# A macaron encoder layer on eight cores: entry norm's sums placed inside the preceding FFN, 256-query exponentials, split down tiles, and a different order of the last stages

## The chip, the cores and the metric

The kernel runs on the 8 cores of one Trainium2 chip. Each core does the whole layer for 2 of the 16 sequences, and the cores do not talk to each other. The metric is the device time of the slowest core, in microseconds (us).

Most executions of a kernel here agree within 0.3% (before the change, 14 of 20 lie from 3009.4 to 3017.6 us). Only fast executions are compared. Even among those, one die is sometimes slightly disturbed (in a fast execution of `a_xycut` one die is at 0.982 to 0.984 and the other at 0.989 to 0.992), and the slowest of eight cores is a noisy statistic. So I also use the **undisturbed die mean**: over all executions of a kernel, I take each die whose four cores all had a granted clock of at least 0.983, and average the spans of its cores. For the three kernels whose last mixer runs without filler to its end (before, `z_xycut`, `a_order`; in the kernel before 75.1 to 78.5 us of it are at a clock of 0.50) the limit is 0.971. I chose both limits after looking at the data; single dies of one kernel then lie within 14 us of each other. n is the number of dies.

The experiments ran in five sets of rounds, and each set ran the kernel before again. Its own die mean differs between the sets, from 3000.1 to 3008.7 us, so a difference of less than about 9 us between kernels of different sets is not shown by the die means alone. Where it matters I also give the difference from the kernel before in the same set.

## The reference, cut to what matters

```python
x = x + 0.5 * swiglu(rms_norm(x), ...)          # FFN1, 1024 -> 2816 -> 1024
proj = rms_norm(x) @ w_in                       # mixer: one projection for all heads
fox = fox_attention(...)                        # 8 heads of 64, causal, F_t - F_s added to the logits
gla = gla_chunk_causal(...)                     # 4 heads, chunked linear attention
x = x + concat(fox, gla) @ w_out
x = x + 0.5 * swiglu(rms_norm(x), ...)          # FFN2
y = rms_norm(x)
```

The input is 16 x 2048 x 1024 in float32. A core handles its 4096 frames as 8 groups (0 to 7) of 512 frames. For each group there is one FFN1, one mixer and one FFN2.

## The kernel before: the parts that matter

Everything is kept transposed: x of one group is 8 tiles of 128 channels x 512 frames, float32, 2 MB, loaded by DMA and later stored as y (another 2 MB). There are three such buffers. A matmul's sum lands in a PSUM bank, and the program lets the next sum start in it only after another engine has emptied (evacuated) it. The weights are not kept on the core: every FFN streams them from memory again, as 352 tiles of 512 KB and 256 of 352 KB in a whole run (sizes after conversion to bf16). Small helpers record all operations in a list. A planner with a model of durations then fixes the order in which each engine runs them, and inserts the semaphore waits. That order is static: an instruction that waits holds up everything behind it on its engine (TensorE for 10.86 us at the entry sums below).

The mixer's attention is slow for TensorE alone, because each pair of matmuls needs an exponential in between (in the bare stretch below, ScalarE is busy for 19.65 of 20 us in which TensorE runs 42 matmuls). So the planner fills it with matmuls of an FFN that is independent of it. An operation has a level, and lower levels are preferred.

```python
def ffn(f, xb, after):
    for half in range(2):
        for cl in range(NC2):                    # 11 chunks of 128 hidden columns
            DMA("pool", ("wgu", wb), wgu[:, wb, :], wgu_d[f][half * NC2 + cl], ...)
            MM(banks[bg][:], [(w4[:, 0, k, :], hF[:, k, :]) for k in range(8)], ...)   # gate
            ...                                  # up, tanh, products: act[:, cl, :]
        for d in range(8):                       # 8 down tiles
            DMA("pool", ("wd", wb), wd[:, wb, :], wd_d[f][half * 8 + d], ...)
            b = nxt("fb", 2)                     # two PSUM banks in turn
            MM(banks[b][:], [(wd[:, wb, c * 128:(c + 1) * 128], act[:, c, :]) for c in range(NC2)], ...)
            STT(x_sb[:, xb, d, :], banks[b][:], 0.25, x_sb[:, xb, d, :], ...)          # add to x
            ...

def ffn1_pre(tg):                                # "entry norm" of a group
    DMA("sp", ("x", xb), x_sb[:, xb, ...], x_d[tg], 1 << 21, ...)
    for k in range(8):
        norm_sq(xb, k, sqM, "sqM", b, k == 7, 0) # square on ScalarE, sum on TensorE
    norm_rstd(rstdF, "rstdF", b, 0)
# ... (mixer, with the attention over 8 heads) ...
ffn1_pre(0)
ffn1(0)
for n in range(NTG):
    if n + 1 < NTG:
        ffn1_pre(n + 1)
    if n >= 1:
        ffn2_pre(n - 1)
    mixer(n)                                     # filled by what follows
    if n >= 1:
        ffn2(n - 1)
    if n + 1 < NTG:
        ffn1(n + 1)
ffn2_pre(NTG - 1)
ffn2(NTG - 1)
```

The softmax here doesn't subtract the row's maximum and nothing guards it: scores larger than these inputs give would overflow.

## Time and profile before

| | before |
|---|---|
| time, median of the first 6 executions | 3013.79 us (3009.38 to 3303.41) |
| undisturbed die mean | 3004.5 us (n = 34; three sets of rounds. Over all five: 3003.1, n = 65) |
| granted clock, mean of a core | 0.973 to 0.976 |
| TensorE busy (profiled core) | 2814 of 3009 us |

TensorE is the limit. At the pace of the FFN matmuls in the trace (0.216 us from start to start for 512 columns) all matmuls together take about 2604 us (an estimate from this pace and the number of columns), which is the floor that no reordering can lower. The rest is what the change aims at.

First, lines of the profile's page (slowest core, core 0): busy time by engine, granted clock and DMA share in 40 slices of the span in tenths, and groups of instructions (count, busy us, mean ns, then the idle time just before them and what ended most of it).

```profile
PE 2813.9 (94%) x13344; PEld 1236.1 (41%) x13344; DVE 1439.4 (48%) x2007; ACT 1251.6 (42%) x3187; POOL 518.2 (17%) x1019
...
PEclk9999989999999999999999999999999999999599
DMA  9978667589776787766877878868887568775066
...
L298 PE MATMUL bank<-hF,wgu 128*128 128x512 bf16 x5632 | 1287.4, 381 | 24.7 <-DMA wgu<-wgu 13.2
...
L298 PE MATMUL bank<-act,wd 128*128 128x512 bf16 x2816 | 641.1, 380 | 19.5 <-DVE act L335 16.2
```

The third digit from the end of the clock string is a 5: one slice of the run, 75 us, is at half clock, and the DMA share of the same slice is 0. FFN matmuls (`hF,wgu`) hardly wait for their weights, 13.2 us in all.

The windows view of the same core shows what that slice is (busy us and instruction count of each engine, then granted clock, DMA share, GB/s):

```profile
2780.00:2800.00 20.00, 19.99 (x42) 4.07 (x41) 6.16 (x4) 19.65 (x76) 1.66 (x4) 0.50 0.00 1
2800.00:2820.00 20.00, 19.99 (x41) 4.03 (x40) 4.04 (x2) 19.64 (x76) 1.67 (x4) 0.50 0.00 0
```

The last mixer has outlived its only filler, and TensorE, at a granted clock of 0.50, and ScalarE run the bare attention, both nearly full by the profile (whose ends of matmuls are modelled).

Now the waits of TensorE, on core 3, which I use because it is an ordinary core (us in total, times, longest):

```profile
PE bank L298 <- ACT sqM L323: 64.5, 25, 11.1
...
PE bank L298 <- DVE act L335: 17.5, 18, 2.0
PE bank L298 <- DVE hM L338: 16.0, 8, 2.3
PE bank L298 <- DMA wgu<-wgu: 11.7, 19, 2.0
```

The largest wait is for the squares of the entry norm (`sqM`). The timeline of TensorE on core 3 shows two of its places (start, duration, then in brackets the idle time before and what ended it):

```profile
42.73 1.10 PE L298 MATMUL bank<-sqM,onesD 128*128 128x512 bf16 x2 [10.86 <-ACT sqM L323]
...
47.99 2.31 PE L298 MATMUL bank<-hF,wgu 128*128 128x512 bf16 x7
...
640.88 1.10 PE L298 MATMUL bank<-sqM,onesD 128*128 128x512 bf16 x2 [10.55 <-ACT sqM L323]
```

At the start, TensorE's queue stands 10.86 us at the entry sums of group 1 although group 0's FFN could run; its first FFN matmul comes at 48 us. At 641 us, in the middle of the program, it stands 10.55 us because x of the next group has not landed (ScalarE's square before it waits 10.80 us for that DMA): the planner placed the sums where its model had the data ready.

### The profile page before, as it was taken

What the parts mean: (1) busy time and instruction counts of PE and PEld (TensorE: products, weight loads), DVE (VectorE), ACT (ScalarE), POOL (GpSimd) and SP (SyncE); (2) the same over time, 40 slices, a digit from 0 to 9 for tenths busy, and PEclk for the clock granted to TensorE, in tenths of its full rate; (3) what the DMA queues carried; (4) which work ended last, traced back from release to release, by engine and by line L of the source; (5) the groups of instructions that cost most, each with busy time, mean ns of one, the idle gap of its engine ahead of it and who ended that gap; (6) DMA issues with size and microseconds to landing.
All of it is one profiled execution on the core that took longest, in us unless ns stands there. A gap on an engine that the chain in (4) does not pass through costs nothing.

```text
span 3008.9 us, 40414 instructions; the slowest of 8 cores (2995.9 to 3008.9 us)
## 1 busy us (share of the span) xinstructions
PE 2813.9 (94%) x13344; PEld 1236.1 (41%) x13344; DVE 1439.4 (48%) x2007; ACT 1251.6 (42%) x3187; POOL 518.2 (17%) x1019
## 2 busy tenths in 40 slices
PE   5999989989999999999999899999999999999988
PEld 1445334334443344433444334533445334443233
DVE  2345745633455444553446635364445554454233
ACT  2132433631248522587324323175132762348711
POOL 1111311211112111111112111122111221111110
PEclk9999989999999999999999999999999999999599
DMA  9978667589776787766877878868887568775066
GB/s 184 144 127 138 115 106 125 97 163 146 122 127 114 137 140 134 119 113 118 141 128 129 157 132 136 138 106 160 142 135 130 88 127 147 131 126 101 13 105 116
DMA packets 118057, 380.24 MB, mean 126 GB/s; under 512 B 13391, under 2 KB 13536, under 8 KB 116960
## 3 DMA queue, kind: packets, MB, share of 16 engines
q0 software_dynamic: 106176, 344.07, 70.1%
q1 hardware_dynamic: 11680, 33.58, 3.4%
q8 instruction: 115, 1.88, 0.2%
q14 instruction: 86, 0.70, 0.1%
HBM read 704.84 MB, written 16.78 MB: 240 GB/s over the span
## 4 chain that ended last, share of the span: by engine, by line
PE 73%; DMA 14%; DVE 6%; issue 4%; ACT 3%; SPq 0%; DVEq 0%; POOL 0%; ACTq 0%; POOLq 0%
PE bank L298 73%; DMA mixw_t<-mixw 6%; DMA wgu<-wgu 4%; DMA x_sb<-x 2%; DMA y<-x_sb 1%; DVE hM L338 1%; DVE x_sb L338 1%; DVE Sst L338 1%; ACT hM L323 1%; DVE hM L689 1%; DMA wd<-wd 1%; ACT L323 1%; DVE Sbf L335 1%; DVE act L335 0%; ACT sqM L323 0%
## 5 line engine op out<-in xcount | busy, mean ns | idle before, releaser
L298 PE MATMUL bank<-hF,wgu 128*128 128x512 bf16 x5632 | 1287.4, 381 | 24.7 <-DMA wgu<-wgu 13.2
L298 PEld LDWEIGHTS bank<-hF,wgu 128*128 128x128 bf16 x5632 | 531.8, 98 | 687.9 <-issue 97.9
L298 PE MATMUL bank<-act,wd 128*128 128x512 bf16 x2816 | 641.1, 380 | 19.5 <-DVE act L335 16.2
L323 ACT ACTIVATE hM<-bank,biasT 128x128 bf16<-128x128 f32 x2176 | 596.6, 400 | 112.0 <-PE bank L298 111.1
L323 ACT ACTIVATE thF<-bank 128x512 f32<-128x512 f32 x352 | 210.6, 600 | 751.3 <-PE bank L298 750.0
L338 DVE SCALAR_TENSOR_TENSOR thF<-thF,bank 128x512 f32<-128x512 f32 x352 | 240.7, 686 | 549.6 <-ACT thF L323 548.5
L298 PEld LDWEIGHTS bank<-act,wd 128*128 128x128 bf16 x2816 | 266.8, 98 | 350.1 <-issue 48.0
L356 POOL DMA_DIRECT2D wgu<-wgu x352 | 190.3, 541 | 1181.6 <-PE bank L298 1178.8
L335 DVE TENSOR_TENSOR act<-bank,thF 128x512 bf16<-128x512 f32 x352 | 242.4, 689 | 238.4 <-PE bank L298 231.8
L338 DVE SCALAR_TENSOR_TENSOR x_sb<-bank,x_sb 128x512 f32<-128x512 f32 x256 | 176.4, 690 | 358.5 <-PE bank L298 357.9
L689 DVE RECIPROCAL hM<-bank 64x512 f32<-64x512 f32 x64 | 214.7, 3355 | 69.6 <-PE bank L298 68.0
L356 POOL DMA_DIRECT2D wd<-wd x256 | 137.5, 537 | 588.2 <-PE bank L298 576.4
L298 PE MATMUL bank<-hM,V 128*128 128x512 bf16 (+3 forms) x640 | 221.3, 374 | 8.1 <-POOL hM L335 4.4
L298 PE MATMUL bank<-QT,KT 64*128 64x512 bf16 (+3 forms) x640 | 221.6, 374 | 0.4 <-ACT hM L323 0.3
L298 PE MATMUL bank<-hM,mixw_t 128*128 128x512 bf16 x896 | 203.0, 379 | 6.4 <-DMA mixw_t<-mixw 5.9
L323 ACT ACT_TABLE_LOAD x99 | 127.0, 1283 | 114.4 <-PE bank L298 108.3
L298 PE MATMUL bank<-mixw_t,hM 128*128 128x256 bf16 x1280 | 150.1, 278 | 18.3 <-DMA mixw_t<-mixw 18.2
L323 ACT ACTIVATE sqF<-x_sb 128x512 bf16<-128x512 f32 x128 | 81.0, 633 | 196.0 <-DVE x_sb L338 195.6
L356 POOL DMA_DIRECT2D mixw_t<-mixw x128 | 68.3, 533 | 507.1 <-PE bank L298 478.6
L323 ACT ACTIVATE sqM<-x_sb 128x512 bf16<-128x512 f32 x128 | 77.3, 625 | 181.3 <-DVE x_sb L335 124.8
L335 POOL TENSOR_TENSOR hM<-hM,mask 128x128 bf16<-128x128 bf16 x256 | 117.0, 467 | 188.8 <-ACT hM L323 184.6
L298 PEld LDWEIGHTS bank<-mixw_t,hM 128*128 128x128 bf16 x1280 | 126.2, 100 | 44.7 <-issue 25.2
(93 smaller groups left out, 1412.3 us busy)
## 6 DMA issues: line engine op xcount, KB each, us to landing
wgu<-wgu POOLq DMA_DIRECT2D x352, 512.0 KB, 6.1
wd<-wd POOLq DMA_DIRECT2D x256, 352.0 KB, 5.6
mixw_t<-mixw POOLq DMA_DIRECT2D x128, 512.0 KB, 6.4
y<-x_sb SPq DMA_DIRECT2D x64, 256.0 KB, 9.0
x_sb<-x SPq DMA_DIRECT2D x7, 2048.0 KB, 14.2
x_sb<-x SPq DMA_DIRECT2D x8, 256.0 KB, 13.6
wmisct<-wmisc POOLq DMA_DIRECT2D x1, 80.0 KB, 14.3
gT<-gains SPq DMA_DIRECT2D x1, 16.0 KB, 24.4
```

Source lines behind the costliest of these rows:

```text
L298: ins = e.matmul(out, lhsT=l, rhs=r, start=s0, stop=s1)
L323: ins = e.activation(out=out, in_=in_, func=func, **kw)
L335: return DVE(lambda e: e.tensor_tensor(out=out, in0=a, in1=b, op=op), free_n(out), reads, writes, rate, eng, level)
L338: return DVE(lambda e: e.scalar_tensor_tensor(out=out, in0=a, scalar=s, in1=b, op0=op0, op1=op1), free_n(out), reads, writes, level=level)
L356: return P.op(eng, lambda e: e.dma_start(out=out, in_=in_), reads, writes, dma_key=key, dur=1000.0 if eng == "pool" else 70.0, lat=100.0, ...
L689: P.op("dve", lambda e, o_=rcp[drow, :], i_=banks[ob][srow, :]: e.reciprocal(out=o_, in_=i_), [], [PS(ob), ("hM", 6), ("hM", 7)], dur=3300 ...
```

## The change

Its intent: TensorE should never stand at an entry sum; the last mixer should have filler to its end; the first down tile should not wait for the last hidden chunk; and ScalarE should issue fewer exponentials. The parts are:

1. **Entry sums.** x of the next group is loaded when the preceding FFN starts, and its sums stand in the middle of that FFN (`middle`). The first weight load waits for x tile 5 of group 0, so that x goes first.
2. **Order.** The last FFN1 precedes the FFN2 of group 5, so the last mixer has two FFN2s as filler instead of one.
3. **Split.** The first two down tiles run 10 of their 11 products each before the last chunk is needed.
4. **Exponentials** cover 256 queries with one bias instead of 128 (this also halves the bias tables).
5. **Output projection.** Every tile takes the head pair that ends last (pair 3) as its last product, and the first two tiles run all their other products before either takes it.

The planner's model of DMA changes too: each of the two queues has its own time line instead of a common one, the planned rate is 0.34 instead of 0.35, and x is planned at 0.15 instead of 0.4.

```diff
-        def ffn(f, xb, after):
+        def ffn(f, xb, after, middle):
...
-                    DMA("pool", ("wgu", wb), wgu[:, wb, :], wgu_d[f][half * NC2 + cl], 1 << 20, writes=[("wgu", wb)])
+                    DMA("pool", ("wgu", wb), wgu[:, wb, :], wgu_d[f][half * NC2 + cl], 1 << 20, writes=[("wgu", wb)],
+                        reads=[("x", 0, 5)] if cnt["wgu"] == 1 else ())
...
+                load(0)
+                load(1)
+                part(0, 0, NC2 - 1)
+                part(1, 0, NC2 - 1)
+                part(0, NC2 - 1, NC2)
+                evac(0)
+                part(1, NC2 - 1, NC2)
+                evac(1)
+                if half == 0 and middle is not None:
+                    middle(bu)
+                for d in range(2, 8):
+                    load(d)
+                    part(d, 0, NC2)
+                    evac(d)
...
-                    ACTV([(Pt[:, r, t * 128 - off:(t + 1) * 128 - off], banks[b][:, t * 128 - off:(t + 1) * 128 - off],
-                           AF.Exp, biasT[:, t, j, h:h + 1], None) for t in range(off // 128, 4)],
+                    spans = [(max(off, t * 256), t * 256 + 256, t) for t in range(off // 256, 2)]
+                    ACTV([(Pt[:, r, a - off:z - off], banks[b][:, a - off:z - off], AF.Exp, biasT[:, t, j, h:h + 1], None)
+                          for a, z, t in spans], [("biasT", t) for _, _, t in spans], [PS(b), ("hM", r)])
...
+            early = [4, 5, 6, 7, 0, 1, 2]        # output projection: head pair 3 last
...
+        order = [("f1", 0), ("f1", 1)]
+        for g in range(NTG - 3):
+            order += [("f2", g), ("f1", g + 2)]
+        order += [("f1", NTG - 1), ("f2", NTG - 3), ("f2", NTG - 2), ("f2", NTG - 1)]
+        for i, (kind, g) in enumerate(order):
+            nk, ng = order[i + 1] if i + 1 < len(order) else (None, None)
+            if nk == "f1":
+                load_x(ng)
+            middle = (lambda b, ng=ng: ffn1_pre(ng, b)) if nk == "f1" else None
...              (run FFN1 or FFN2 of g)
+            m = g if kind == "f1" and g < NTG - 1 else NTG - 1 if (kind, g) == ("f2", NTG - 3) else None
+            if m is not None:
+                mixer(m)
```

## The prediction

> **What bounds the kernel now.** TensorE. The engine table has it busy 2814 of 3009 us (94%). [...] By start-to-start times in the trace, about 175 us more is a per-switch cost (0.32 us instead of 0.21 for each QK or PV matmul), which the change leaves. Some 240 us is stall:
>
> 1. Start. The first FFN matmul is at 45.4 us. The list by time shows hF of group 0 begun at 31.7, but TensorE's queue stands at the entry-norm sums of group 1 (10.15 us wait for its x, then 5 us of sums).
> 2. Entry norms in the way near 375-391, 630-645 and 1725-1740 us: about 38 us with the half clock after them (ACT sqM is PE's largest wait, 65.7 us, most of it item 1).
> 3. Tail, 2766-2873 us: no FFN work is left beside the last mixer. The windows view gives granted clock 0.50, PE 19.99 and ACT 19.65 of 20 us busy: both are limits. Then 4.6 us wait for the last reciprocal, 24 us of half-fed output projection, 7.3 us for the next norm. Stall about 52 us. [...] 0.50 after the waits at 2766-2776.
> 4. First down tile waits for the last act chunk: 1.2 us, 13 times, 16 us.
> 5. Output projection waiting for the last head or its weights: 7 x 1.3 us.
> 6. Weight loads of the mixer, some 30 us: not touched.
>
> **What the change does.**
> - Item 1: sums of group 1 move into the middle of FFN 0; the first FFN weight load waits for x tile 5, so x lands earlier. Weights then come later and the DMA share is already about 1.0: gain 8 us.
> - Item 2: x is loaded one FFN ahead, its sums stand among FFN matmuls: 33 us.
> - Item 3: FFN1 of the last group precedes an FFN2, so the last mixer has two FFN2s (about 115 us each) as filler instead of one: 48 us.
> - Item 4: ten of eleven products of two down tiles (4.3 us) run before the last chunk is needed: 15 us.
> - Item 5: head pair 3 last: 6 us.
> - 256-query exponentials: 2176 of 128 columns (0.26 us apart) become 1024 of 256 and 128 of 128. [...] ACT falls from 1250 to about 1100 us. PE waits for them only 3.7 us in all, so nothing is gained unless the tail stays bare.
> - Cost: x loads (2 MB) share DMA with FFN weights at a share of 0.86-0.97: 5 to 15 us.
>
> Sum about 110 us less cost: **2903 us**, range 2868 to 2942. Chances: faster 0.93, same 0.06, slower 0.01.
>
> **What would show it.** PE's wait on ACT squares of entry norms below 35 us, all before 45 us; no stretch over 20 us at clock 0.5; mean clock above 0.98; first FFN matmul before 40 us; PE's wait on DVE act below 4 us; ACT busy near 1100 us; wgu waits up from 13 us.
>
> **What would make it wrong.** TensorE's order is static: where x lands after its planned time, the sums stall again. Contention of the x load. If the last mixer still outlives its filler, half of the gain goes. [...]

## The result, and the profile after

| | before | after |
|---|---|---|
| median, all executions | 3013.78 us (20, up to 3407.58) | 2962.35 us (10, 2958.55 to 3263.24) |
| ratio of the fast runs | 1 | 0.9828, 95% interval 0.9818 to 0.9838 |
| undisturbed die mean | 3004.5 us (n = 34) | 2950.8 us (n = 18) |
| granted clock, mean of a core | 0.973 to 0.976 | 0.984 to 0.989 |

A ratio here and below is the mean time of one kernel's fast runs over that of the other's in the same rounds, so it is not quite the ratio of the medians. The kernel after is 1.7% faster. The gain is 51 us of the medians, 54 of the undisturbed dies (52 by the ratio). The prediction had 111 and its range excluded the result.

The same lines of the page, after. The profiled core is core 6, the slowest by 15 us; the other seven are within 2941 to 2953.

```profile
PE 2784.0 (94%) x13328; PEld 1235.7 (42%) x13328; DVE 1430.8 (48%) x1991; ACT 1098.1 (37%) x2161; POOL 513.8 (17%) x1019
...
PEclk9999999999999999999999999999999999999999
DMA  8978767598775787746977788766888647854695
...
L300 PE MATMUL bank<-hF,wgu 128*128 128x512 bf16 x5632 | 1300.6, 384 | 71.8 <-DMA wgu<-wgu 53.3
...
L300 PE MATMUL bank<-act,wd 128*128 128x512 bf16 x2816 | 645.8, 380 | 19.7 <-DVE x_sb L340 17.2
```

The half-clock slice is gone, and the DMA works to the end. But two lines have not become smaller. The wait of FFN matmuls for their weights has gone from 13.2 to 53.3 us. The idle time before the down tiles is 19.7 us instead of 19.5: what they wait for has changed from the last hidden chunk (`act`) to `x_sb`, the evacuation of a bank.

The windows view of the place where the bare attention stood (here core 6, 40 us each) has it now among FFN matmuls at full clock:

```profile
2700.00:2740.00 40.00, 40.00 (x163) 14.60 (x162) 14.72 (x14) 23.16 (x61) 7.72 (x16) 1.00 0.48 80
2740.00:2780.00 40.00, 40.00 (x179) 16.63 (x177) 19.55 (x21) 16.64 (x39) 5.98 (x12) 1.00 0.64 108
```

The waits of TensorE on core 3, after:

```profile
PE bank L300 <- DMA wgu<-wgu: 48.8, 25, 7.2
PE bank L300 <- ACT sqF L325: 27.5, 8, 8.6
PE bank L300 <- DVE hM L340: 20.5, 7, 7.6
...
PE bank L300 <- DVE x_sb L340: 17.2, 14, 2.5
```

And its timeline at the places where it stood at entry sums before:

```profile
35.35 12.10 PE L300 MATMUL bank<-hF,wgu 128*128 128x512 bf16 x48 [7.38 <-DVE hF L340]
54.61 9.68 PE L300 MATMUL bank<-hF,wgu 128*128 128x512 bf16 x34 [7.16 <-DMA wgu<-wgu]
...
626.25 11.90 PE L300 MATMUL bank<-hF,wgu 128*128 128x512 bf16 x48 [4.04 <-DMA wgu<-wgu]
...
643.15 11.98 PE L300 MATMUL bank<-hF,wgu 128*128 128x512 bf16 x48 [5.00 <-DMA wgu<-wgu]
```

The first FFN matmul comes at 35 us instead of 48, and gives 7.16 us back at 54.6, where the weights are late. Near 640 us the 10.55 us at the entry sum has become 4.04 and 5.00 us at weights. The windows view of core 3 has the reason for suspicion: the DMA is full there, as it was in the kernel before (0.97 and 1.02 in the same stretches).

```profile
600.00:620.00 20.00, 16.34 (x76) 7.07 (x75) 11.33 (x17) 8.07 (x10) 2.64 (x5) 1.00 0.98 177
620.00:640.00 20.00, 14.12 (x59) 5.75 (x56) 5.51 (x8) 2.39 (x4) 2.11 (x4) 0.91 1.02 221
```

The DMA view of the same two stretches splits this by queue (packets, MB, share of 16 engines; q0 brings the weights, q1 moves x and y):

```profile
q0 software_dynamic: 648, 1.93, 67.5%
q1 hardware_dynamic: 877, 1.61, 30.6%
...
q0 software_dynamic: 497, 1.84, 57.7%
q1 hardware_dynamic: 415, 2.56, 44.4%
```

The weights lie in memory as float32 and arrive as bf16 (the page counts 344 MB that arrive by q0 and 705 MB read), so each of their bytes that arrives is two that are read. In the fastest 20 us of weights alone that I found (core 6, from 2550 us) 174 GB/s arrive, about 348 GB/s read (an estimate). In the two stretches above, about 273 and 312 GB/s are read or written (estimates). They stay below that rate, though the DMA engines' time is full (0.98 and 1.02).

**Where TensorE's time goes.** From the starts of the matmuls in the trace I worked out a sum for each kernel. Each gap between two starts is cut into the dense pace; the usual extra of that pair of neighbours (a switch from a QK to a PV matmul, say; the median of such gaps); the part that falls into a stretch at half clock; and a stall, put down to the matmul that it precedes. Figures are us, the mean of the six cores whose records are complete. The columns after the first two belong to the experiments below.

| | before | after | z_xycut | a_xycut | e_order | a_nosplit | a_bal2 | b_bn | c_att_bn |
|---|---|---|---|---|---|---|---|---|---|
| until the first FFN matmul | 46.7 | 35.0 | 47.5 | 34.7 | 45.9 | 35.2 | 35.0 | 35.5 | 34.9 |
| stall before entry and other norm sums | 29.2 | 4.8 | 10.0 | 4.8 | 38.6 | 4.7 | 5.4 | 4.6 | 4.6 |
| before FFN gate/up (mostly weights) | 31.2 | 70.9 | 29.6 | 43.1 | 34.7 | 61.9 | 62.0 | 60.3 | 52.1 |
| before down tiles | 21.8 | 21.8 | 21.6 | 21.8 | 30.8 | 30.9 | 9.7 | 5.7 | 5.0 |
| before the mixer's first matmul (norm) | 16.3 | 21.0 | 16.3 | 20.7 | 14.4 | 21.2 | 21.0 | 20.8 | 20.3 |
| before the output projection | 16.2 | 2.7 | 11.3 | 2.1 | 6.7 | 4.5 | 3.0 | 5.3 | 3.8 |
| half clock | 46.9 | 23.1 | 40.9 | 18.8 | 19.0 | 20.9 | 23.7 | 21.2 | 20.3 |
| switches | 169.0 | 157.9 | 169.4 | 157.3 | 161.5 | 161.2 | 159.4 | 154.7 | 154.8 |
| total to the last matmul | 2991.2 | 2938.6 | 2961.0 | 2907.1 | 2944.2 | 2938.7 | 2919.1 | 2908.0 | 2901.6 |

Between before and after, 24 us of sums, 12 at the start, 24 of half clock, 13.5 at the output projection and 11 of switches are gone, and 40 us before FFN matmuls and 5 before the mixer's norm have come. That nets 40 of the 52.6 us between the totals; about 12 more lie in lines that are not shown. So the expected gain went to two places: weights that come late, and a split that gained nothing.

The row "before FFN gate/up" is not weights alone. By the waits view, in the mean of the eight cores, the wait for weights has grown from 11.7 to 50.0 us, and the wait for `thF`, a product on VectorE, from 1 to 10.9. About 4 us of the latter are a wait for x in another dress. The list by time of core 0 in the kernel after:

```profile
2084.93 1.15 ACT L325 ACTIVATE sqF<-x_sb 128x512 bf16<-128x512 f32 x2 [10.47 <-DMA x_sb<-x]
2085.99 1.06 ACT L325 ACTIVATE thF<-bank 128x512 f32<-128x512 f32 x2
2086.67 0.69 DVE L340 SCALAR_TENSOR_TENSOR thF<-thF,bank 128x512 f32<-128x512 f32 x1 [9.64 <-ACT thF L325]
2087.50 4.83 PE L300 MATMUL bank<-hF,wgu 128*128 128x512 bf16 x11 [6.10 <-DVE thF L340]
```

ScalarE stands 10.47 us at the entry square of group 7, whose x has not landed. Behind it in ScalarE's fixed order stands the tanh of the FFN, behind that VectorE's product, and behind that TensorE. ScalarE waits there for 9.2 to 10.6 us on each of the eight cores, and on five of them TensorE loses 4.8 to 7.0 us. So this entry norm still holds TensorE up, by way of ScalarE. In `a_xycut` below, where x is cut, these waits are gone.

### The profile page after: what moved, and what is told of

It reads as the page before. It is cut to its first block, busy times and chain, and to the rows that moved or that the text cites. A ratio compares the mean times of both kernels' runs of the same rounds, so it can differ in the third digit from the quotient of the medians.

```text
span 2968.0 us, 39375 instructions; the slowest of 8 cores (2941.3 to 2968.0 us)
## 1 busy us (share of the span) xinstructions
PE 2784.0 (94%) x13328; PEld 1235.7 (42%) x13328; DVE 1430.8 (48%) x1991; ACT 1098.1 (37%) x2161; POOL 513.8 (17%) x1019
## 4 chain that ended last, share of the span: by engine, by line
PE 75%; DMA 14%; DVE 5%; issue 3%; ACT 2%; POOL 0%; SPq 0%; DVEq 0%; POOLq 0%; ACTq 0%
PE bank L300 75%; DMA wgu<-wgu 7%; DMA mixw_t<-mixw 5%; DVE hF L340 1%; DVE hM L340 1%; DMA x_sb<-x 1%; DVE x_sb L340 1%; DMA y<-x_sb 1%; DVE Sst L340 1%; ACT L325 1%; DMA wd<-wd 0%; DVE Sbf L337 0%; ACT hM L325 0%; ACT rstdM L325 0%; ACT rstdY L325 0%
## 5 line engine op out<-in xcount | busy, mean ns | idle before, releaser
L300 PE MATMUL bank<-hF,wgu 128*128 128x512 bf16 x5632 | 1300.6, 384 | 71.8 <-DMA wgu<-wgu 53.3
L300 PE MATMUL bank<-act,wd 128*128 128x512 bf16 x2816 | 645.8, 380 | 19.7 <-DVE x_sb L340 17.2
L325 ACT ACTIVATE hM<-bank,biasT 128x256 bf16<-128x256 f32 (+1 forms) x1152 | 439.5, 469 | 179.6 <-PE bank L300 178.5
L325 ACT ACTIVATE sqF<-x_sb 128x512 bf16<-128x512 f32 x192 | 117.2, 629 | 388.8 <-DVE x_sb L340 210.5
L716 DVE RECIPROCAL hM<-bank 64x512 f32<-64x512 f32 x64 | 214.7, 3355 | 50.6 <-PE bank L300 48.8
L300 PE MATMUL bank<-hM,V 128*128 128x512 bf16 (+3 forms) x640 | 206.6, 353 | 2.8 <-POOL hM L337 1.6
L300 PE MATMUL bank<-QT,KT 64*128 64x512 bf16 (+3 forms) x640 | 207.8, 354 | 1.2 <-DVE Sst L340 0.7
L300 PEld LDWEIGHTS bank<-mixw_t,hM 128*128 128x128 bf16 x1280 | 125.4, 99 | 40.1 <-issue 21.8
L300 PEld LDWEIGHTS bank<-hM,mixw_t 128*128 128x128 bf16 x896 | 86.0, 98 | 115.7 <-issue 15.0
## 6 DMA issues: line engine op xcount, KB each, us to landing
x_sb<-x SPq DMA_DIRECT2D x8, 256.0 KB, 14.4
```

The costliest lines, as they stand in the source:

```text
L300: ins = e.matmul(out, lhsT=l, rhs=r, start=s0, stop=s1)
L325: ins = e.activation(out=out, in_=in_, func=func, **kw)
L716: P.op("dve", lambda e, o_=rcp[drow, :], i_=banks[ob][srow, :]: e.reciprocal(out=o_, in_=i_), [], [PS(ob), ("hM", 6), ("hM", 7)], dur=3300 ...
```

## The experiments

18 experiments ran (17 kernels, one of them twice). All give correct results except `a_xycut` and `z_xycut`, which move less data on purpose (their results are not numbers). "Die" is the undisturbed die mean, and "own rounds" what it is less the die mean of the kernel before in the same set of rounds, with the number of the set. Diffs are against the kernel after, unless said otherwise.

| label | what it is | ratio to before [95%] | die (n) | own rounds (set) |
|---|---|---|---|---|
| before | | 1 | 3004.5 (34) | 0 |
| after | | 0.9828 [0.9818, 0.9838] | 2950.8 (18) | -52, by the ratio |
| a_order | order undone | 1.0014 [0.9967, 1.0062] | 3002.4 (3) | -6.3 (1) |
| e_order | order, exponentials and output projection alone | 0.9854 [0.9827, 0.9881] | 2959.4 (7) | -42.5 (4) |
| a_nosplit | no split | 0.9870 [0.9834, 0.9906] | 2950.9 (4) | -52.5 (2) |
| a_exp128 | exponentials of 128 | 0.9860 [0.9807, 0.9912] | 2956.1 (4) | -52.6 (1) |
| a_nox5 | first weight load does not wait | 0.9832 [0.9807, 0.9857] | 2953.4 (8) | -46.8 (3) |
| a_xycut | after, x and y traffic cut | 0.9744 [0.9706, 0.9782] | 2917.7 (5) | -91.1 (1) |
| z_xycut | before, x and y traffic cut | 0.9886 [0.9865, 0.9908] | 2971.2 (7) | -30.8 (4) |
| b_paced | x and y paced along the FFN | 0.9856 [0.9827, 0.9884] | 2956.9 (7) | -46.5 (2) |
| c_att | x and y moved into attention | none | 2949.7 (6) | -50.4 (3) |
| a_bal | split balanced | none | 2941.9 (2) | -66.8 (1) |
| a_bal2 | the same again | 0.9771 [0.9751, 0.9790] | 2931.9 (10) | -69.2 (5) |
| a_nd | planned norm time 0.80 us | 0.9812 [0.9794, 0.9830] | 2945.4 (8) | -56.6 (4) |
| b_bn | balanced, norm time | 0.9733 [0.9708, 0.9757] | 2918.5 (7) | -81.7 (3) |
| b_paced_bal | paced, balanced | 0.9805 [0.9785, 0.9825] | 2938.9 (8) | -64.5 (2) |
| b_pbn | paced, balanced, norm time | none | 2921.9 (7) | -81.5 (2) |
| e_order_bn | e_order, balanced, norm time | 0.9760 [0.9734, 0.9786] | 2928.4 (9) | -72.7 (5) |
| c_att_bn | c_att, balanced, norm time | 0.9703 [0.9681, 0.9725] | 2913.7 (9) | -86.4 (3) |
| c_abn_nox2 | c_att_bn without the move of x of group 2 | 0.9717 [0.9695, 0.9739] | 2914.7 (7) | -87.3 (4) |

"None" means no ratio, as too few executions were fast.

### Which part gained what

My theory after the two traces: the order of the last stages made the whole gain; the entry sums removed a stall that came back at weights; the split gained nothing. The rival: each part gained a share, and all were smaller than predicted.

**The order undone.**

```diff
-        order += [("f1", NTG - 1), ("f2", NTG - 3), ("f2", NTG - 2), ("f2", NTG - 1)]
+        order += [("f2", NTG - 3), ("f1", NTG - 1), ("f2", NTG - 2), ("f2", NTG - 1)]
...
-            m = g if kind == "f1" and g < NTG - 1 else NTG - 1 if (kind, g) == ("f2", NTG - 3) else None
+            m = g if kind == "f1" else None
```

> The changed kernel with the last FFN1 back behind the FFN2 of group 5. If the filler of the last mixer is worth what I predicted: 30 to 50 us slower than 2962 (about 3000), with a bare attention stretch at granted clock 0.5 back near the end (somewhat shorter than the 78 us of the kernel before, as exponentials are 256 wide). If the tail's gain came from the exponentials: less than 15 us slower.

The kernel is back at the time of before: ratio 1.0014, die 3002.4. The order is worth 3002.4 - 2950.8 = 52 us when it is added last (46 if each kernel is set against the kernel before in its own rounds).

**The order alone** (with the exponentials, the output projection, and the planner's new model of DMA except for x's rate): no split, no wait of the first weight load, and the entry sums at the mixer's head again.

```diff
         def ffn1_pre(tg):
             xb = tg % 3
+            if tg:
+                load_x(tg)
+            b = 3 + nxt("mb", 3)
             for k in range(8):
-                norm_sq(xb, k, sqF, "sqF", b, k == 7, None)
+                norm_sq(xb, k, sqM, "sqM", b, k == 7, 0)
...
-            middle = (lambda b, ng=ng: ffn1_pre(ng, b)) if nk == "f1" else None
+            middle = None
...
+            if kind == "f1" and g < NTG - 1:
+                ffn1_pre(g + 1)
```

> The kernel after with only its order of the last stages and its 256-query exponentials and output-projection order left: entry sums back at the head of the mixer as in the kernel before, no split of the down tiles, no wait of the first weight load. Theory (start, entry sums and split are worth nothing net, and the order is worth the whole gain): undisturbed die 2945 to 2958, as the kernel after (2950.8); PE's wait for the entry squares back near 25 us, its wait for FFN weights back near 30 to 40. Rival (entry sums and start do save their 40 us, and the order alone is worth less than it seems because what it saves overlaps them): 2970 or higher.

It is 45 us faster than before on an undisturbed die (42.5 in its own rounds), and 8.6 us slower than after. The theory's number (2945 to 2958) was just missed: the three other parts together are worth 9 us, not nothing, and not the 40 of the rival. Its wait for weights was forecast near 30 to 40 us and is 17.0 on core 3. The waits of TensorE on core 3 of `e_order`:

```profile
PE bank L300 <- ACT sqM L325: 74.4, 17, 13.6
PE bank L300 <- DVE act L337: 26.4, 26, 2.3
PE bank L300 <- DMA wgu<-wgu: 17.0, 17, 4.1
PE bank L300 <- DVE hM L340: 14.0, 7, 2.3
```

**No split.**

```diff
-                part(0, 0, NC2 - 1)
-                part(1, 0, NC2 - 1)
-                part(0, NC2 - 1, NC2)
+                part(0, 0, NC2)
                 evac(0)
-                part(1, NC2 - 1, NC2)
+                part(1, 0, NC2)
                 evac(1)
```

> The changed kernel without the split of the first two down tiles (11 products of tile 0, then 11 of tile 1, as before). My theory that the split only moved the wait: time within 6 us of 2962, the wait on DVE x_sb replaced by a wait on DVE act of about the same sum (15 to 20 us). If the split had gained what I predicted: 12 to 18 us slower.

2950.9 against 2950.8: the split is worth nothing. The waits of core 3 in `a_nosplit` show 25 waits for the last hidden chunk, where the kernel after has 14 for the bank, and weights later by less:

```profile
PE bank L300 <- DMA wgu<-wgu: 36.8, 27, 7.0
...
PE bank L300 <- DVE act L337: 25.5, 25, 2.3
...
PE bank L300 <- DVE x_sb L340: 3.1, 2, 2.3
```

In the table of stalls the split takes 9 us away before the down tiles (30.9 to 21.8), and 9 us more stand before FFN matmuls (61.9 to 70.9).

`a_nosplit` and `e_order` differ in the entry sums and the start only (and in the rate at which the planner expects x to land), so they show what those do: 34 us fewer before sums (38.6 to 4.7) and 11 at the start, but 27 more before FFN matmuls and 7 more before the mixer's norm. Of 45 us removed, 34 are back in these two lines. By the waits view, in the mean of the cores, the wait for weights is 36.0 us in `a_nosplit` and 18.5 in `e_order`, and 8.5 us in `a_nosplit` are the wait at ScalarE for x that is shown above.

**128-query exponentials again.**

> The changed kernel, its exponentials issued as 128-query instructions again (same bias per 256 queries, same numbers). My prediction's view (ScalarE no limit while FFN work fills in): time within 10 us of 2962, ACT busy back near 1250 us. Rival theory (256-query exponentials make attention shorter, leave less of the FFNs as filler and more bare FFN stretch, which is where weights starve): TensorE's wait for wgu falls by 15 us or more and the time falls too.

Its die mean is 5 us above that of the kernel after, but in its rounds the kernel before was slow as well (3008.7), and against that it gains 52.6 us, as much as the kernel after. So no effect is shown. ScalarE's busy time fell by 154 us through the change (1251.6 to 1098.1), and the kernel's time shows nothing of it. The prediction's figure for ScalarE, about 1100 us, was the author's estimate, and it came true: exponentials follow each other at 0.250 us with 128 columns (before) and at 0.357 with 256 (after).

**The first weight load does not wait for x tile 5.**

```diff
-                        reads=[("x", 0, 5)] if cnt["wgu"] == 1 else ())
+                        )
```

> The changed kernel without the wait of the first FFN weight load for x tile 5. TensorE's order is the same. If that wait speeds up x as intended: first FFN matmul later than 35 us by 2 to 5 us, but weights earlier, so that the 6 to 7 us wait for wgu near 50 us shrinks; net within 5 us of 2962. If the wait is harmful (it also holds back four wd loads behind it): 3 to 8 us faster.

The first FFN matmul comes at 41.2 us instead of 35.0, but the weights later on are less late (stall before them 64.8 instead of 70.9), and the kernel is slower by 2.6 us only (5 in its own rounds, 1 by the ratios), which is not clear of noise. So an earlier start by six microseconds is not shown to be worth six. A likely reason, not tested, is that the DMA has the same work to do before about 70 us in either order.

### Is the lateness of the weights the x and y traffic?

**The traffic cut in the kernel after.** x of groups 3 to 7 loads one of eight tiles, y of groups 0 to 6 stores an eighth of each tile. TensorE's order of instructions stays the same.

```diff
+                P.op("sp", lambda e: e.dma_start(out=x_sb[:, xb, 0, :], in_=x_d[tg, :, 0:T]), (),
+                     [("x", xb, k) for k in range(8)], dma_key=("x", xb), ...)          # groups 3 to 7
...
+                w = T if tg == NTG - 1 else T // 8
+                P.op("sp", lambda e, k=k, w=w: e.dma_start(out=y_d[tg, :, k * T:k * T + w], in_=x_sb[:, xb, k, 0:w]), ...)
```

> The changed kernel with the same instruction order, but x of groups 3 to 7 is loaded for one tile of eight, and y of groups 0 to 6 is stored for one column block of eight (wrong result on purpose). Theory 1 (DMA supply: the x loads and y stores take the DMA engines from the FFN weight stream in the bare FFN stretches, so the stalls at the entry norms were moved, not removed): TensorE's waits for wgu fall from 53 us to below 25 us, the stalls near 610-650, 1705-1730, 2065-2090 and 2810-2830 us go, and the time falls by 25 to 45 us to about 2920-2935. Rival (static order or evacuation latency makes the new stalls): time within 8 us of 2962, stalls where they were.

33 us faster (2917.7), and 28 of them are stall before FFN matmuls (70.9 to 43.1). In the waits of core 3, the wait for weights halves from 48.8:

```profile
PE bank L300 <- DMA wgu<-wgu: 25.0, 23, 6.4
```

**The control: the same cut in the kernel before.** Without it, the run above proves only that traffic costs, not that the change made it cost.

> The kernel BEFORE with the same cut of its x and y traffic as the earlier run that cut the kernel after (x of groups 3 to 7 an eighth, y of groups 0 to 6 an eighth; wrong results on purpose). It is the control of that run, in which the kernel after gained 33 us on an undisturbed die. Theory (the kernel after pays for traffic that its own placing put against FFN weights): the kernel before gains clearly less, 10 to 20 us (undisturbed die 2985 to 2995 instead of 3004.5), and it gains it at its entry norms, not before its FFN1 and FFN2 weights. Rival (any kernel of this shape gains the same from so much less traffic): 30 us or more, 2975 or lower.

The rival's number came: the kernel before gains 33 us as well (3004.5 to 2971.2). Only the place is as the theory said: the gain lies at the entry sums (29.2 to 10.0), the half clock (46.9 to 40.9) and the output projection (16.2 to 11.3), and nothing of it before FFN weights (31.2 to 29.6). The timeline of core 3 in `z_xycut`, at the sums that waited 10.55 us in the kernel before, and its waits:

```profile
624.40 0.90 PE L298 MATMUL bank<-sqM,onesD 128*128 128x512 bf16 x2 [0.56 <-ACT sqM L323]
...
625.65 0.90 PE L298 MATMUL bank<-sqM,onesD 128*128 128x512 bf16 x2 [0.35 <-ACT sqM L323]
```

```profile
PE bank L298 <- ACT sqM L323: 48.6, 24, 10.3
...
PE bank L298 <- DMA wgu<-wgu: 8.6, 18, 1.1
```

So the x and y traffic has a bill of about the same size in both kernels, for about two thirds of it (the cut takes 55% of x and 77% of y). That both die means give 33 is in part luck: in their own rounds the cuts gain 39 us (after) and 31 (before), and the totals of the traces differ by 31.5 and 30.2. The kernel before pays it where TensorE waits for x, and the kernel after where it waits for weights. By moving the sums, the change moved the bill; it did not cancel it. The page gives the size of the traffic: the x and y queue takes 3.4% of 16 engines' span, about 102 us of the whole DMA, so two thirds are some 67 us (an estimate), about half of which TensorE feels.

**Can pacing avoid it?** If bursts were the cause, 256 KB pieces spread along an FFN would help. x and y go tile by tile, each released by an FFN chunk; TensorE's order is the same.

```diff
                     TT(act[:, cl, :], banks[bu][:], thF[:, r, :], ALU.mult, [("th", r)], [PS(bu), ("act", cl)], level=0)
+                    for fn in feed.pop((me, half * NC2 + cl), ()):
+                        fn(("act", cl))           # one x tile or one y tile
```

> The changed kernel with TensorE's order untouched; only when x and y move differs: y of groups 0 to 3 goes out one 256 KB tile per FFN chunk in the first half of the next FFN, x of groups 3 to 6 comes in the same way in its second half, y of groups 5 and 6 over the whole next FFN, x of group 2 during the second half of the second FFN1. Group 4 to 7 hand-over is left as it was. Theory 1 (bursts of 4 MB beside a weight stream that already fills 85 to 97% of the DMA): stalls before wgu fall from about 71 us (mean core) to 45-55, half clock falls by 5-10 us, time falls by 15 to 35 us to about 2930-2945. Rival (the total DMA work in bare FFN stretches is too much whatever its pace): stalls before wgu stay within 8 us of 71, spread out; time within 8 us of 2962.

It is 6 us slower. On core 3 the stalls are spread (about 8 near 608 to 646, 7 near 683 to 706, 7 near 1059 to 1086, and so on) and their sum grew, from 70.9 to 76.0. The theory of the burst falls. In stretches of FFN alone the weights take a DMA share of 0.78 to 0.97 (in the kernel after 0.78 to 0.90 on core 3 at 400, 420 and 1000 us, 0.87 to 0.96 on core 6 from 80 to 170; in the kernel before up to 0.97), so there is little room at any pace.

**Can the traffic go where the DMA has room?** In attention stretches the share is about a half (0.48 and 0.54 on core 3 at 500 and 560 us). y of groups 0 and 3 and x of groups 2, 3 and 6 now wait for the mixer's state (`("S", 0)`), and the entry sums concerned move to the FFN's second half.

```diff
+            for st_ in held.pop(tgg - 2, ()):
+                st_([("S", 0)])                   # the held y stores
+            if tgg - 2 in HELD:
+                load_x(tgg + 1, [("S", 0)])
+            if tgg == 0:
+                load_x(2, [("S", 0)])
```

> The changed kernel with three transfers moved to where the DMA has room: y of groups 0 and 3 and x of groups 3 and 6 (4 MB each pair) wait until the attention of the mixer two groups on begins (DMA share about 0.45 there), their entry sums move to the second half of that FFN2; x of group 2 waits for the attention of mixer 0. Same bursts, other place. Theory now (after pacing failed): the bare FFN stretches have no DMA room at any pace, so only another place helps: the stalls near 605-645 and 1705-1735 us go, stall before wgu falls from 71 to 45-52 us (mean core), half clock by some 5 us, time falls by 20 to 30 us to about 2933-2942, mean of an undisturbed die from 2951 to 2921-2932. Rival (the weight stream itself starves there, x and y or not, as in the parts that the cut of x and y left): less than 8 us.

Alone it gives 1 us, which is nothing clear of noise, and its theory (20 to 30 us) fell. The old places did shrink (on core 3 from 13.4 to 4.0 near 612 us, and to nothing near 1720), but new stalls came at 288 to 299 us (8.1), 858 (4.1) and 1944 (3.9). On top of the two edits below it gives 5 (2918.5 to 2913.7, in the same rounds). Taking back the one move that made the stall at 290 us changes nothing (2914.7): on core 3 the stall at 290 us goes, and the old one at 48 us returns (6.3 us):

> The fastest kernel so far (x and y of four groups in attention stretches, balanced split, norm time; undisturbed die 2913.7) with the load of group 2 back where the kernel after has it. Theory (that one move cost 8 us, the new stall near 290 us, and brought back about 8 at 53 us): equal, 2911 to 2917. Rival (moving it was a net loss): 2904 to 2909, a ratio near 0.968.

### Why the split gained nothing, and what does

In the kernel after, tile 2 writes the bank that tile 0 used. That bank is free only after tile 0's evacuation on VectorE (0.69 us, group mean), and between the last product of tile 0 and the first of tile 2 there is one matmul, 0.22 us. A split that leaves more of tile 1 for later should hide the evacuation:

```diff
                 part(0, 0, NC2 - 1)
-                part(1, 0, NC2 - 1)
+                part(1, 0, 5)
                 part(0, NC2 - 1, NC2)
                 evac(0)
-                part(1, NC2 - 1, NC2)
+                part(1, 5, NC2)
                 evac(1)
```

> The changed kernel with the split of the first two down tiles rebalanced: 10 products of tile 0, 5 of tile 1, the last of tile 0, then 6 of tile 1, so that tile 0 is evacuated while tile 1 still runs. Theory: the split only moved the wait from the last act chunk to the bank of tile 2 (DVE x_sb, 14 waits, 17.2 us); then this wait falls below 5 us and the time falls by 12 to 20 us. Rival: other stalls take it up, less than 5 us.

The first run had one fast execution of four, and its profile has 160 us at a clock of 0.81 on four cores. It gave no ratio, and I took its 9 us by die means (2941.9) for the gain. It was run again with more rounds:

> The same kernel as the earlier run of the balanced split alone, which gave one fast run of four and a profile with 160 us at clock 0.81 on four of its cores. The norm time alone gave 5 us (2945.4), both edits together 32 (2918.5). Theory (the two do not add: the split alone gives 9 us, and together they remove a stall that each alone leaves): undisturbed die 2938 to 2945. Rival (they add, and the first figure of 9 us came from disturbed runs): 2921 to 2928, so that 23 to 30 us are the split's.

The second run: 2931.9, so the balanced split gives 19 us, between my theory (9) and the rival (23 to 30), and within the 12 to 20 that I had expected at first. The first figure did not come from disturbed executions, as both its dies were undisturbed. In its rounds the kernel before was slower too: set against that, the two runs gain 66.8 and 69.2 us and agree, which makes the split worth 15 to 17. The wait for the bank has gone from 17.2 to 4.0 us, by the waits of core 3:

```profile
PE bank L300 <- DVE x_sb L340: 4.0, 9, 2.3
```

In the table the stall before the down tiles falls by 12 us and that before FFN matmuls by 9. About 4 of the 9 are the wait at ScalarE for the x of group 7, which no longer reaches TensorE there. Why the weights are less late is not shown.

**A planning time.** The planner takes 613 ns for a 512-column VectorE operation; the trace has 686 to 690 ns. One edit plans 800 ns for the norm tiles alone (`.dur = 800.0` in `norm_h`). I meant it for the wait before the mixer's norm, first with the paced kernel:

> The same plus the balanced split of the first two down tiles. Expected from the balanced split alone (wait on DVE x_sb 17.2 us fell to 4.0 us on core 3): 8 to 14 us below the paced kernel, about 2920-2935. If the gain of the balance is eaten by weight waits (a faster TensorE asks for weights earlier): less than 4 us below.

> Candidate best: paced x and y, balanced split, and the scheduler told that one tile of a norm takes VectorE 0.80 us (trace: 0.746) instead of 0.613, so that it places the first matmul of the mixer after more FFN filler (stall before it: 21 us in 8). If that wait is one of planned order: stall before wmisc falls from 21 to below 10 us, time 5 to 12 us below the paced and balanced kernel, about 2910-2925. If not: equal within 4 us.

> The changed kernel with the balanced split and the longer norm time, x and y moved as in the changed kernel. Tells what pacing was worth in the fastest kernel so far (undisturbed die 2922): if pacing costs 3 to 6 us as it did alone, this one has 2916-2919 on an undisturbed die; if pacing helps when TensorE is denser, 2925-2930.

> The kernel after with nothing but the planner's time of a norm tile set to 0.80 us. The balanced split and this together gave 32 us on an undisturbed die, the balanced split alone 9. Theory (the two effects add): 23 us, undisturbed die 2925 to 2931, ratio near 0.976. Rival (the planned time only helps with the balanced split, whose down tiles it shortens): 2940 or higher.

`b_paced_bal` (2938.9) gains 18 us on `b_paced` in the same rounds (8 to 14 were expected), as the balanced split does elsewhere, and `b_pbn` (2921.9, few fast runs) another 17. `b_bn`, without pacing, is at 2918.5; in their own rounds the two gain the same (81.5 and 81.7), so pacing is worth nothing here. The norm time alone gives 5 us (`a_nd`; the theory of 23 fell), and 13 on top of the balanced split (2931.9 to 2918.5). These compare different rounds, and the two do not quite add. Its target did not move: the stall before the mixer's norm is 20.8 us in `b_bn`, against 21.0. What moved is the stall before down tiles (9.7 to 5.7) and the switches (159.4 to 154.7). The gain is measured, and my reason for it fell. The edit changes the planned order in many places, and which of them counts is open.

**Are the entry sums worth more once the down tiles do not stall?**

> The kernel with the order alone (entry sums at the mixer's head, no wait of the first weight load), now with the balanced split and the norm time of 0.80 us. It tells whether the entry sums placed in the FFN and the earlier start are worth anything once the down tiles no longer stall. Theory (they are worth the same 9 us that they are worth without it, 2959.4 against 2950.8): undisturbed die 2924 to 2930, slower than the 2918.5 of the kernel after with the same two edits. Rival (they are worth nothing there, the DMA time is only paid at another place): 2914 to 2921.

2928.4 against 2918.5: 10 us, as the theory had it (9 without these two edits). In their own rounds the difference is 9. The value of the entry sums and the start is small and steady.

### A better version

> The same with the balanced split and the longer norm time in the scheduler. If the gains add: another 12 to 25 us below, about 2910-2925, undisturbed die about 2900-2915.

`c_att_bn` is the fastest, with `c_abn_nox2` not told apart from it: ratio 0.9703, three fast executions at 2922.0, 2924.6 and 2925.6 us, correct. It beats the kernel before by 3.0% and the kernel after by 37 us on an undisturbed die, 19 from the balanced split, 13 from the norm time, 5 from the attention moves. Its wait for weights on core 3:

```profile
PE bank L300 <- DMA wgu<-wgu: 35.6, 27, 10.7
```

In the mean of the cores this wait is 27.9 us, and another 10 us are lost behind ScalarE, which waits for x there as in the kernel after. That is the next thing to mend.

## Why the prediction was wrong, point by point

The signs that the prediction named came true: the wait for entry squares was 28.3 us on the profiled core (24 of them before 45 us), no stretch over 20 us at clock 0.5, mean clocks above 0.98, the first FFN matmul at 35 us, no wait for `act` above 4 us, ScalarE busy 1098 us, and more waiting for weights. The time did not follow, because most of the signs said that old stalls had gone, and none said how much may come back.

| step of the prediction | predicted, us | measured on undisturbed dies, us | by |
|---|---|---|---|
| order of the last stages (item 3) | 48 | 52 added last (46 in own rounds); 45 together with item 5 and the exponentials | a_order, e_order |
| output projection (item 5) | 6 | not run alone; the stall fell from 16.2 to 2.7 | table of stalls |
| 256-query exponentials | 0 | none shown | a_exp128 |
| start and entry sums (items 1, 2), less "5 to 15" for DMA | 41 - 10 = 31 | 9, with the split, which is worth 0 | e_order, a_nosplit |
| split of two down tiles (item 4) | 15 | 0 | a_nosplit |
| sum | 100 | 54 | |

- **The tail was right.** Mechanism and size held: 48 predicted, 43 to 52 measured.
- **The step that failed most is the cost, "x loads share DMA with FFN weights: 5 to 15 us".** The contention was named, but its term was mis-sized. The stall before FFN matmuls grew by 40 us instead of 5 to 15 (the wait for weights by itself by 38); `a_nosplit` against `e_order` puts 27 of it, and 7 more before the mixer's norm, on the entry sums and the start. The prediction read the DMA share of 0.86 to 0.97 as nearly enough. It counted x loads only, and it took the stall at the sums for a matter of order, when much of it was the DMA's time. `z_xycut` shows the latter: 19 of 29 us at the sums go when the traffic goes. The risk that the prediction named, x landing after its planned time, also came true in one place, at ScalarE near 2080 us.
- **The split, "ten of eleven products run before the last chunk is needed: 15 us", was wrong in mechanism.** It looked at the wait that the split removes, and not at the next thing that the tile needs: the bank. The wait changed from `act` (16.2 us) to `x_sb` (17.2 us). Against the changed kernel without the split (25.5 us at `act` on core 3) it did fall, but the stall before FFN matmuls grew by as much.
- **The start** came 12 us earlier (8 predicted), but 7 us came back near 54 us, likely because the same bytes must land before that point (not tested). `a_nox5` gives the wait of the first weight load 3 us, not clear of noise.
- **An arithmetic slip.** 3013.8 less 110 is 2903.8: the number does not have the cost subtracted that the text names. Subtracting 10 gives about 2914, which is still too low by 48.
- **The wait before the mixer's norm**, 16.3 to 21.0 us, was not foreseen: its longest on core 3 is 7.6 us instead of 2.3, at 369 us, where the second mixer starts. I did not test the cause.
- **The half clock after stalls** that the prediction read from the trace (0.50 after the waits at 2766 to 2776 us; on core 0 from 2771 us, after a wait of 2.34 us) is there after the change too. The kernel after still has 12 to 18 stretches of 3.4 to 13.7 us at 0.50 on each core, which cost 23 us. On core 3 each of them but the last (the end of the run) begins at a wait of TensorE, and at seven of these 13 the wait is only 2.2 to 2.7 us long.

What stays open: why weights are less late with either no split or a balanced one; what the planner's new DMA model does by itself; which reordering makes the norm time's 5 to 13 us; and the value of the output projection's order by itself.

## What to carry to other kernels

A wait on a compute step behind a DMA may be the DMA's bill presented elsewhere: before pricing its removal, cut the traffic in the kernel before and in the kernel after, because only the pair tells a saved cost from a moved one. When a wait is taken away, ask what the same instruction needs next (here the PSUM bank, one matmul later), and leave enough independent work to cover that as well. Write down for a change not only what should vanish from the profile, but how large each line that may grow can be before the gain is gone.

## What the traces show of the clock and the DMA

- In the kernel before, bare attention kept TensorE busy 19.99 of every 20 us by the profile, and the clock stayed at 0.50 for 75.1 to 78.5 us on end on every core. The matmuls themselves started 0.54 us apart there, against 0.32 us for the same pairs at full clock. Mixed with FFN matmuls (the kernel after) the same attention ran at 1.00. So "busy" in the profile did not go with full clock here. Waits of 2.2 to 2.7 us were followed by half clock (core 3 of the kernel after).
- All eight cores of the kernel after ran at a mean clock of 0.984 to 0.989 in the profiled execution. A clock of 0.81 appeared in some executions only, such as 160 us in `a_bal` on cores 0, 1, 6 and 7 (mean clock 0.976 to 0.979, the other four 0.986 to 0.989), which are two cores of each die and not a whole die.
- Here a DMA share of 0.78 to 0.97 in FFN stretches meant that the x and y traffic came out as stall at both paces tried: 31 to 39 us for about 67 us of DMA time (an estimate).
